# A hybrid S5, attention and expert layer: feature-major prologue, R on VectorE, x_mid stored and scaled by GpSimd

## The chip, the core and the metric

The kernel runs on one core of a Trainium2 chip. The metric is the device time of one execution in microseconds; less is better. TensorE (PE in the rows) does the matrix products, VectorE (DVE), ScalarE (ACT) and GpSimd (POOL) the element work, SyncE (SP) issues most transfers. An engine runs its instructions in the order in which they stand in its program; semaphores order the engines against each other.

## What is computed

```python
h  = modulate(rmsnorm(x), sh1, sc1)           # sh1, sc1, g1, sh2, sc2, g2 = silu(c) @ w_ada + b_ada
u, q_a, kv_a, k_r, gates = split(h @ w_in)    # for the 512 latent tokens x and the 256 context tokens ctx
# (a) two-way diagonal S5 scan over u (32 groups of 16 channels, 64 complex states each), then GLU
# (b) latent attention, 8 heads, over context and latent tokens
x_mid = x + g1 * (sigmoid(gates) * branches) @ w_out
h2  = modulate(rmsnorm(x_mid), sh2, sc2)
aff = softmax(h2 @ w_router)                  # 16 experts; each takes its 64 best tokens
out = x_mid + g2 * expert_choice_ffn(h2)      # SwiGLU with FF = 2816, scattered back by token
```

All in float32, D_MODEL = 1024, one sample. The experts' weights are about 554 MB of the 643 MB that the kernel moves.

## The kernel before

**Prologue.** Tokens lie as 8 slots `l` by 96 chunks (32 of ctx, 64 of x). SP loads `pk` (small constants), `X` (four tiles of 96 partitions, token-major), `craw` and `braw`, then the 16 pieces of `w_ada` for the first third (`wada`), then the first blocks of `w_in` (`win_u`, 128 columns each). ACT sums the squares of each row, DVE scales `X` by the norm, PE transposes it (L354, `xT`) into `xTa`, `xTb` (x, feature-major) and `hc` (ctx). PE forms the modulation `ada` (L191), `ada_end` moves it to columns (`adar`, `adac`, `acol`, `ab1`), and L632 to L643 make `h = x*a + b` per 128 features `k`, split as `hx` = (hi, lo) for products of three matmuls (`mm3`, L122 to L124). A weight block is split likewise into `ws` by `win_prep` (ACT, then one DVE subtraction).

**In-projection and S5.** Four `u` blocks (24 matmuls of 512 columns, and 16 of ctx, `pc`, L662) feed the S5 part; the other 21 blocks are "fills", put between the S5 steps to keep PE busy. The S5 loop runs over four group blocks `gb`. Per block: `s5_P` (tables `PT`, ten instructions, GpSimd), `s5_R` (powers `R`, about 20 instructions, GpSimd), `s5_Q` (tables `Q`, ten instructions, DVE), `s5_K` (matmuls `pkc` on `PT`, a round trip through `kd` in HBM, tile `M`), `s5_B` (transposes `pbt` of `Q`), `s5_V` (matmuls `pv`, DVE products with `R`, a scan, `Xc`), `s5_Y` (matmuls `py` on `M`, `PT`, `Xc`) and `s5_T`. `PT` and `R` have two buffers each, and P and R of block gb+2 follow Y of block gb on GpSimd. The stretch is under `manual_schedule`: written order is engine order. The in-projection ends at 307 us.

**Attention and router.** After MLA and attention, `pxm` gives `x_mid` in four token tiles `xm` and two column halves `n`. Each half is transposed (`pxt`, `xmT`) and multiplied with the router weights (`prt`: 4 products with a 128x128 stationary `xmT` and 16 columns). Tile by tile ACT stores `x_mid` to `out` (L1402, two DMAs a tile on ACT's queue) and then scales `xm` in place by the norm (L1405), for which it waits until the stores have landed. Then comes the top-k (8 rounds on DVE), and `pxg` gathers the rows of each expert from the scaled `xm`.

**Experts.** SP issues the weights of the 16 experts (L1450) into a ring of ten 2 MB slots, from 534 us on; each slot waits until PE has read its old content. The first expert's `pgu` starts at 625.73 us.

Of the kernel before, what the change touches and what calls it, by code (L numbers as in the profile page):

```python
# [18 lines left out]
D = 1024  # L19
SEQ = 512  # L20
# [36 lines left out]
def hybrid_block(ctx: ExitStack, tc: tile.TileContext, A, out, dbg=None, stop=99):  # L57
# [118 lines left out]
    win = A["w_in"].rearrange("(k p) n -> p k n", p=128)  # L176
    wada = A["w_ada"].rearrange("(k p) n -> p k n", p=128)
# [26 lines left out]
    def wada_src(t, kn, kh, q):  # L204
        return wada[:, kn * kh:kn * kh + kn, (4 * t + q) * 512:(4 * t + q + 1) * 512]


    pha = ph1.enter_context(ExitStack())
    for n, k in (("xx", 4), ("jk", 1)):
        cur[n] = pool(n, pha, bufs=k)  # L210
    man = ph1.enter_context(ExitStack())
    man.enter_context(tc.manual_schedule())
    xv = A["x"].rearrange("(c l) d -> c l d", l=L)
    cv = A["ctx"].rearrange("(c l) d -> c l d", l=L)
    X = []
    for j in range(4):
        t = tl("xx", f"X{j}", [NCH, 2, D])
        dma(t[0:NCX], cv[:, 2 * j:2 * j + 2, :])
        dma(t[NCX:NCH], xv[:, 2 * j:2 * j + 2, :])
        X.append(t)  # L220
    craw = cst("craw", [128, 2, 32, 16], p="early")
    dma(craw, A["ssm_c"])
    braw = tl("qq", "braw", [128, 2, 32, 16])
    dma(braw, A["ssm_b"])
    hc = tl("hxp", "hc", [128, 8, 256])
    wt = {}

# [12 lines left out]
    wada_load(2, [("m4", 0), ("m4", 0), ("rr", 0), ("rr", 0)])  # L240

# [55 lines left out]
    ssx = cst("ssx", [NCH, L])  # L297
    rstd = cst("rstd1", [NCH, L])
    for l in range(L):
        jk = tl("jk", "sqj", [NCH, D])  # L300
        S.activation(jk, X[l // 2][:, l % 2, :], AF.Square, accum_out=ssx[:, l:l + 1])
# [30 lines left out]
    def xnorm(hf):  # L332
        l0 = 4 * hf
        vx = sm("vx", [NCH, 4])
        ts(vx, ssx[:, l0:l0 + 4], 1.0 / D, EPS)
        yield
        yield from rsqrt_g(rstd[:, l0:l0 + 4], vx, [NCH, 4])
        for l in range(l0, l0 + 4):
            ts(X[l // 2][:, l % 2, :], X[l // 2][:, l % 2, :], rstd[:, l:l + 1])
            yield  # L340

    xt = []

    def xt_half(hf):
        if not hf:
            xt.extend([tl("pt", "xTa", [128, 4, 512]), tl("bt", "xTb", [128, 4, 512])])
        for kp in range(4):
            p = pw("xT")
            pv = p[:, :, 0:4 * NCH].rearrange("p k (l c) -> p k l c", l=4)
            k = 2 * kp  # L350
            for kk in range(2):
                for l in range(4):
                    lx = 4 * hf + l
                    T.transpose(pv[:, kk, l, :], X[lx // 2][:, lx % 2, 128 * (k + kk):128 * (k + kk) + 128],  # L354
                                ident[0:NCH, 0:NCH])
            S.copy(xt[k // 4][:, k % 4:k % 4 + 2, 256 * hf:256 * hf + 256].rearrange("p k (l c) -> p k l c", l=4),
                   pv[:, :, :, NCX:])
            V.tensor_copy(hc[:, k:k + 2, 128 * hf:128 * hf + 128].rearrange("p k (l c) -> p k l c", l=4),
                          pv[:, :, :, :NCX])
            for _ in range(4):  # L360
                yield
# [17 lines left out]
    lp = tl("uu", "lp", [128, 2, 9, 32])  # L379
# [7 lines left out]
    def powers():  # L387
        cm1 = sm("cm1", W32)
        stt(cm1, sh, -2.0, sh, ALU.mult, ALU.mult)
        yield  # L390
        ts(cb, cm1, 1.0, None, ALU.add)
        yield
        mul(nre, em1, cb)
        yield
        add(nre, nre, cm1)
        mul(lp[:, 0, 1], ex, cb)
        yield
        cmul(lp[:, :, 2:3], lp[:, :, 1:2], lp[:, :, 1:2], [128, 2, 1, 32], dtl)
# [5 lines left out]
        for o, m0, rev in ((lt_, 0, 1), (lq, 1, 0)):  # L404
            for dr in range(2):
                src = lp[:, :, m0:m0 + 8].rearrange("p r m (g d q) -> p g d r q m", d=2, q=4)[:, :, dr]
                dst = o.rearrange("p r (g d q) m -> p g d r q m", d=2, q=4)[:, :, dr]
                for g in range(4):
                    V.tensor_copy(dst[:, g], src[:, g, :, :, ::-1] if dr == rev else src[:, g])
                    yield  # L410
            if o is lt_:
                ts(lt_[:, 1], lt_[:, 1], -1.0)
# [71 lines left out]
    rr(expm1_parts(za, ex, em1), trig(), late_by(5, xnorm(0)))  # L484
    S.activation(sh, br, AF.Sin)
    S.activation(ch, ab, AF.Sin)
    rr(xnorm(1), late_by(2, powers2()), late_by(2, powers()), late_by(8, xt_half(0)))
    wada_load(3, [("zz", 0), ("xc", 0), ("xx", 1)])
    pada = pg("ada0")
    for k in range(2):  # L490
        ada_part(pada, k, [wt[0, q][:, k] for q in range(4)])
    rr(xt_half(1), rot(), late_by(8, bbar_g()))
    for k in range(2, 8):
        ada_part(pada, k, [wt[k // 2, q][:, k % 2] for q in range(4)])

# [104 lines left out]
    def win_load():  # L600
        if nxt["load"] < len(order):
            f, b = order[nxt["load"]]
            nxt["load"] += 1
            w = tl("raw", f"win_{f}{b}", [128, 8, 128])
            c = base[f] + 128 * b
            dma(w, win[:, :, c:c + 128])
            wins.append(w)

    def win_prep():

        if nxt["prep"] < len(order):
# [6 lines left out]
            if fb == ("u", 0):  # L618
                return
# [4 lines left out]
    for _ in range(4):  # L624
        win_load()
    wkr = tl("kr", "wkr", [128, 8, 32])
    dma(wkr, win[:, :, 1152:1184])
    ada_end(0, pada, tl("dt", "adar0", [128, 512]), win_prep)
# [88 lines left out]
    def f_kr():  # L719
# [12 lines left out]
        V.tensor_copy(kr4[:, 0:512], px)  # L732
        V.tensor_copy(kr4[:, 512:768], pc)
# [3 lines left out]
        V.tensor_copy(krt, pk_)  # L737
# [104 lines left out]
    win_prep()  # L842
    s5_Q(0)
    o = f_u(0)
    win_prep()
    u_out(0, *o)
# [792 lines left out]
```

## Time and profile before

| | us |
|---|---|
| median of 3 runs (range) | 1921.36 (1916.97 to 1926.43) |
| the profiled execution: its own time | 1919.85 |
| its span | 1918.1 |
| PE busy / DVE / ACT / POOL | 1633.8 / 531.5 / 320.7 / 209.9 |
| in-projection ends | 307 |
| top-k starts | 601.7 |
| first expert matmul | 625.73 |

The span is cut into stretches by what runs: 0 to 59 us prologue, 59 to 108 us the `u` blocks, to 307 us the S5 loop with fills, to 495 us MLA and attention, to 601 us `pmo`, `pxm` and router, to 626 us top-k and first gather, then the experts. The share of the longest chain is 43% PE, 36% DMA, 8% DVE. In a row of a timeline the brackets at the end tell how long the engine stood idle before it and what ended that.

### The profile page before, as it was taken

Reading aid. Unit: us, or ns where it says so; the run is one execution under the profiler, and the core shown is the slowest. Engines: PE = TensorE matmul, PEld = TensorE weight load, DVE = VectorE, ACT = ScalarE, POOL = GpSimd, SP = SyncE. Lnnn points to the kernel's source line nnn. Section 1 sums busy time; section 2 is a strip of 40 time slices with the busy share of each in tenths; the row PEclk is TensorE's granted clock in tenths of the full one; section 3 lists DMA queues with packets and bytes.
Section 4 is the critical chain, followed back from the end, with each engine's and each line's share of the span. In section 5 each row is a group of like instructions: output and inputs, shape, how many; then the busy total and the mean of one; then the engine's idle time right before and its main releaser. Section 6 shows DMA issues by size and latency. Waiting matters only on the chain.

```text
span 1918.1 us, 20921 instructions
## 1 busy us (share of the span) xinstructions
PE 1633.8 (85%) x8660; PEld 791.5 (41%) x8660; DVE 531.5 (28%) x1180; ACT 320.7 (17%) x593; POOL 209.9 (11%) x218
## 2 busy tenths in 40 slices
PE   3798999999995988888888888888888788888886
PEld 2586778755573333333333333323223232332322
DVE  7877665675745101011000100001000010100000
ACT  3422225364421000000000000000000000000000
POOL 3667200231110000000000000000000000000000
PEclk8899999999997999999999999999999999999999
DMA  9243353525539899999999999999999999999996
GB/s 316 57 141 111 105 189 133 170 97 201 157 90 401 363 422 426 422 427 420 422 427 422 421 426 422 426 423 423 425 421 427 421 427 421 420 428 421 427 422 281
DMA packets 108654, 642.56 MB, mean 335 GB/s; under 512 B 10256, under 2 KB 45072, under 8 KB 73232
## 3 DMA queue, kind: packets, MB, share of 16 engines
q1 hardware_dynamic: 105040, 631.79, 81.2%
q0 software_dynamic: 2880, 7.34, 1.7%
q10 hardware_dynamic: 640, 2.10, 0.3%
q8 instruction: 68, 1.11, 0.2%
q14 instruction: 26, 0.21, 0.0%
HBM read 623.93 MB, written 17.27 MB: 334 GB/s over the span
## 4 chain that ended last, share of the span: by engine, by line
PE 43%; DMA 36%; DVE 8%; issue 5%; ACT 3%; POOL 2%; POOLq 0%; ACTq 0%; SPq 0%; DVEq 0%
DMA wgu<-in_w_e_gu 18%; PE pgu L1505 14%; DMA wd<-in_w_e_down 10%; PE pdn L1520 8%; DMA wd<-in_w_e_down_end 6%; PE pxg L1462 2%; PE po L1263 1%; DVE hd L94 1%; PE px L122 1%; PE px L124 1%; PE px L123 1%; ACT hd L1507 1%; PE ada L191 1%; PE phT L1512 1%; PE py L801 1%
## 5 line engine op out<-in xcount | busy, mean ns | idle before, releaser
L1505 PE MATMUL pgu<-wgu,xe 128*64 128x512 f32 (+1 forms) x3072 | 644.9, 559 | 27.5 <-DMA wgu<-in_w_e_gu 26.0
L1505 PEld LDWEIGHTS pgu<-wgu,xe 128*64 128x64 f32 x3072 | 219.9, 137 | 426.5 <-issue 351.1
L1520 PE MATMUL pdn<-wd,hT 128*64 128x512 f32 x1408 | 357.5, 645 | 34.5 <-ACT hT L1514 34.5
L94 DVE TENSOR_TENSOR hd<-hd,pgu 64x512 f32<-64x512 f32 x96 | 61.9, 645 | 994.3 <-ACT hd L1507 994.3
L1507 ACT ACTIVATE hd<-pgu 64x512 f32<-64x512 f32 x96 | 53.3, 556 | 951.5 <-PE pgu L1505 951.5
L1520 PEld LDWEIGHTS pdn<-wd,hT 128*64 128x64 f32 x1408 | 110.9, 146 | 214.2 <-issue 163.6
L1539 POOL DMA_INDIRECT out<-ye,sidx x16 | 24.9, 1556 | 1340.7 <-DVE ye L112 1340.7
L1512 PE MATMUL phT<-pk,hd 64*128 64x64 f32 x352 | 42.1, 236 | 126.7 <-DVE hd L94 126.7
L1512 PEld LDWEIGHTS phT<-pk,hd 64*128 64x128 f32 x352 | 29.0, 138 | 204.3 <-DVE hd L94 204.3
L122 PE MATMUL px<-hx,ws 128*128 128x512 f32 x200 | 81.1, 406 | 6.3 <-ACT hx L637 6.3
L123 PE MATMUL px<-hx,ws 128*128 128x512 f32 x200 | 80.1, 400 | 3.5 <-DVE hx L94 3.4
L124 PE MATMUL px<-hx,ws 128*128 128x512 f32 x200 | 79.5, 398 | 1.4 <-DVE ws L94 1.4
L1462 PE MATMUL pxg<-xm,oh 128*64 128x512 f32 x256 | 75.3, 609 | 0.6 <-DVE oh L94 0.6
L1514 ACT COPY hT<-phT 128x256 f32<-128x256 f32 x96 | 34.1, 355 | 119.2 <-PE phT L1512 119.2
L122 PEld LDWEIGHTS px<-hx,ws 128*128 128x128 f32 x200 | 38.4, 192 | 15.3 <-ACT hx L637 6.4
L123 PEld LDWEIGHTS px<-hx,ws 128*128 128x128 f32 x200 | 38.1, 190 | 14.7 <-DVE hx L94 7.6
L124 PEld LDWEIGHTS px<-hx,ws 128*128 128x128 f32 x200 | 38.2, 191 | 10.2 <-DVE ws L94 2.5
L1466 DVE COPY xg<-pxg 128x256 f32<-128x256 f32 x16 | 6.8, 424 | 127.1 <-ACT xg L1465 127.1
L1462 PEld LDWEIGHTS pxg<-xm,oh 128*64 128x64 f32 x256 | 30.6, 140 | 21.1 <-issue 19.4
L1233 DVE TENSOR_REDUCE mx<-ps 128x1 f32<-128x768 f32 x32 | 30.5, 954 | 27.7 <-PE ps L124 25.0
L354 PE MATMUL xT<-pk,X 96*128 96x96 f32 x64 | 11.5, 348 | 29.1 <-DMA craw<-in_ssm_c 18.7
L191 PE MATMUL ada<-wada,scv 128*32 128x512 f32 x192 | 34.1, 675 | 0.0
(471 smaller groups left out, 1724.5 us busy)
## 6 DMA issues: line engine op xcount, KB each, us to landing
wgu<-in_w_e_gu SPq DMA_DIRECT2D x176, 2048.0 KB, 37.9
wd<-in_w_e_down SPq DMA_DIRECT2D x80, 2048.0 KB, 37.9
wada<-in_w_ada SPq DMA_DIRECT2D x16, 1024.0 KB, 7.7
wd<-in_w_e_down_end SPq DMA_DIRECT2D x16, 1024.0 KB, 36.8
wada<-in_w_ada SPq DMA_DIRECT2D x16, 512.0 KB, 10.6
win_g<-in_w_in SPq DMA_DIRECT2D x16, 512.0 KB, 4.3
gs<-gt SPq DMA_DIRECT2D x16, 256.0 KB, 2.0
g<-gs SPq DMA_DIRECT2D x16, 256.0 KB, 3.2
```

Of the source, the lines that this page charges most:

```text
L94: (e or V).tensor_tensor(o, a, b, op=op)
L122: T.matmul(o, a[0], b[0], start=first, stop=False)
L123: T.matmul(o, a[0], b[1], start=False, stop=False)
L124: T.matmul(o, a[1], b[0], start=False, stop=last)
L191: T.matmul(p[32 * q:32 * q + 32, :], scv[:, k].rearrange("p s n -> p (s n)"), w[q], start=(k == 0), stop=(k == 7))
L1233: V.tensor_reduce(mx, p[:, 0:768], AX.X, ALU.max, negate=True)
L1462: T.matmul(px[64 * h:64 * h + 64, :], oh[:, t], xms[t][:, 512 * h:512 * h + 512], start=(t == 0), stop=(t == 3))
L1505: T.matmul(p[64 * j:64 * j + 64, :fn], xe[:, k, :], wt_[8 * j + k], start=(k == 0), stop=(k == 7))
L1507: S.activation(hd[:, :fn], p[0:64, :fn], AF.Silu)
L1512: T.transpose(ph[:, b, :], hd[:, 128 * b:128 * b + 128], ident[0:64, 0:64])
L1514: S.copy(hT[:, :n], ph[:, :n])
L1520: T.matmul(po[64 * h:64 * h + 64, :], hT[:, b, :], w[:, 512 * h:512 * h + 512], start=(f0 == 0 and b == 0), stop=(f0 + 128 * b == FF - 128))
```

## The change

The host lays out x and ctx feature-major (`xt`, `ct`) and `w_ada`, `w_in` in blocks that are contiguous per partition. The transposes go; the norm comes from ACT squares, DVE sums, six matmuls `pssx` with a column of ones, and six matmuls `rb` that spread 1/rms over the partitions. `h` is then made per `k` from `xt`, `ab1` and `rb`, and the blocks u0 and u1 run together, `k` by `k`. R goes from GpSimd to DVE, behind Q; `PT` and `R` have one buffer, so P(gb+1) follows Y(gb). One fill stands ahead of the loop. In the router the weights are the stationary operand, in four column groups. `x_mid` is stored and scaled by GpSimd.

```diff
-    X = []
-    for j in range(4):
-        t = tl("xx", f"X{j}", [NCH, 2, D])
-        dma(t[0:NCX], cv[:, 2 * j:2 * j + 2, :])
-        dma(t[NCX:NCH], xv[:, 2 * j:2 * j + 2, :])
+    xt = [tl("pt", "xTa", [128, 4, 512]), tl("bt", "xTb", [128, 4, 512])]
+    for i in range(2):
+        for j in range(2):
+            k = 2 * j
+            dma(xt[i][:, k:k + 2, :], A["xt"][i, :, k:k + 2, :])
+        dma(hc[:, 4 * i:4 * i + 4, :], A["ct"][:, 4 * i:4 * i + 4, :])
...
+    win_load()
+    wada_load(3, ["m4", "m4", "zz", "xc"])
+    win_load()
+    win_load()
+    win_load()
+    braw = tl("qq", "braw", [128, 2, 32, 16])
+    dma(braw, A["ssm_b"])
...
+    for t in range(6):
+        T.matmul(rb[:, t // 4, 128 * (t % 4):128 * (t % 4) + 128], rstd[:, t:t + 1].to_broadcast([128, 128]), ident,
+                 start=True, stop=True)
...
+    h = modulated(0)
+    for k in range(8):
+        hi, lo = hxs(k)
+        S.activation(hi, h, AF.Identity, bias=ab1[:, 1, k, 0:1])
+        hn = modulated(k + 1) if k < 7 else None
+        if k:
+            hc_mod(k - 1)
+        stt(lo, h, ab1[:, 1, k, 0:1], hi.bitcast(F32), ALU.add, ALU.subtract)
+        h = hn
+        for j in range(2):
+            mm3(pf[:, j, :], [first[j][0][:, i, k, :] for i in range(2)], hxs(k), k == 0, k == 7)
...
     for gb in range(4):
         U, rt = us_.pop(gb)
+        s5_K(gb)
+        if gb < 3:
+            s5_bd(gb + 1)
         Xc = s5_V(gb, U, rt)
...
         if gb < 3:
             s5_Q(gb + 1)
+            s5_R(gb + 1)
         yb = s5_Y(gb, U, Xc)
         if gb < 3:
             us_[gb + 1] = s5_U(gb + 1)
-            s5_bd(gb + 1)
-        if gb < 2:
-            s5_P(gb + 2)
-            s5_R(gb + 2)
+            s5_P(gb + 1)
...
-            prt = pa("prt", (128, 16))
-            if n:
-                T.matmul(prt, ident, lg[:, t, :], start=True, stop=False)
+            prl = pa("prl", (128, 128))
             for k in range(4):
-                T.matmul(prt, xt_[:, k, :], wr[:, 4 * n + k, :], start=(n == 0 and k == 0), stop=(k == 3))
+                T.matmul(prl[32 * k:32 * k + 32, :], wr[:, 4 * n + k, :], xt_[:, k, :], start=True, stop=True)
...
+            prt = pa("prt", (128, 32))
+            T.matmul(prt, lgp[:, t], P("stack"), start=True, stop=True)
...
-                S.dma_start(ov[2 * t + i], xm[64 * i:64 * i + 64])
+                dmr(ov[2 * t + i], xm[64 * i:64 * i + 64])
 
     for t in range(4):
-        S.activation(xms[t], xms[t], AF.Copy, scale=inf[:, t, 1:2])
+        ts(xms[t], xms[t], inf[:, t, 1:2], e=G)
```

On PE the program began with the transposes between the modulation's products; these are its rows from the last transposes to the first block (`ada` the modulation, `adac` its columns, `px` a block).

```order
L354 MATMUL xT<-pk,X_152 128x96 x2
L191 MATMUL ada_427<-wada_166,scv 32x512 x2
L191 MATMUL ada_427<-wada_169,scv 32x512 x2
...
L191 MATMUL ada_427<-wada_424,scv 32x512 x2
L199 MATMUL adac_693<-pk,adar_689 128x8 x4
L122 MATMUL px<-hx_702,ws 128x512
```

The same place now: the sums `pssx` stand first, `rb` in the middle of the modulation.

```order
L370 MATMUL pssx<-ones,acc 128x1 x6
L190 MATMUL ada_432<-wada_164,scv 32x512 x2
L190 MATMUL ada_432<-wada_166,scv 32x512 x2
...
L513 MATMUL rb<-pk,rstd 128x128 x6
L190 MATMUL ada_432<-wada_172,scv 32x512 x2
...
L198 MATMUL adac_507<-pk,adar_505 128x8 x4
L123 MATMUL px_523<-hx_521,ws 128x512
```

The 64 transposes are gone, and the first block waits on `hx` after the same two steps of the modulation.

On DVE, in the first turn of the S5 loop, Q of block 1 stood ahead of the evictions of a fill (`kvo`) and of the gelu (`gl`).

```order
L94 TENSOR_TENSOR Q<-bbar,lq 128x1024
L94 TENSOR_TENSOR qu<-bbar,lq 128x512
L94 TENSOR_TENSOR Q<-Q,qu 128x512
L112 SCALAR_TENSOR_TENSOR kvo<-px,pk,kvo 128x512
L112 SCALAR_TENSOR_TENSOR kvo<-pc,pk,kvo 128x256
```

Now R of block 1 stands between them (`e` holds the powers that it multiplies with); 21 rows, of which these are the last.

```order
L604 COPY R<-e_221 128x16
...
L94 TENSOR_TENSOR cm_u<-R,e_221 128x256
L94 TENSOR_TENSOR cm_w<-R,e_221 128x256
L94 TENSOR_TENSOR R<-cm_u,cm_w 128x8x16 x2
L94 TENSOR_TENSOR cm_u<-R,e_221 128x512
L94 TENSOR_TENSOR cm_w<-R,e_221 128x512
L94 TENSOR_TENSOR R<-cm_u,cm_w 128x8x32 x2
```

What follows on DVE in that turn (`kvo`, the gelu, the next `ws`) moved behind R.

On ACT, in the router, the stores and the scaling stood between the steps that the next tile needs (`xg` squares of a half, `xmT` its transposes, `inf` the softmax).

```order
L1402 DMA out<-xm_4864 64x1024
L1393 ACTIVATE inf,res<-rlt,rmx 128x16
L1405 ACTIVATE xm_4863<-xm_4863,inf 128x1024
L1405 ACTIVATE xm_4864<-xm_4864,inf 128x1024
L1368 ACTIVATE xg_5290,ss_4874<-xm_4865 128x512
L1402 DMA out<-xm_4865 64x1024 x2
L1405 ACTIVATE xm_4865<-xm_4865,inf 128x1024
```

Now they are the last rows of GpSimd ahead of the scatter.

```order
L94 TENSOR_TENSOR wos<-w_out,wos 128x2048 x4
L1431 DMA out<-xm_4782 64x1024 x2
L107 TENSOR_SCALAR xm_4782<-xm_4782,inf 128x1024
L1431 DMA out<-xm_4783 64x1024 x2
L107 TENSOR_SCALAR xm_4783<-xm_4783,inf 128x1024
...
L107 TENSOR_SCALAR xm_4785<-xm_4785,inf 128x1024
L1568 DMA out<-ye,sidx 1024x512 x16
```

On ACT the squares of tile 3 (`xg` on the last `xm`) no longer stand behind the scaling of tiles 1 and 2; on GpSimd the stores of tile t+1 stand behind the scaling of tile t.

## Rows read from the trace of the kernel before

**Rows 1.** The chain that ended last: start us, us, what (router to first expert).
```profile
584.65 10.44 DMA out<-xm
...
617.38 5.34 PE pxg L1462 x16
...
625.73 10.51 PE pgu L1505 x46
```

**Rows 2.** Busy time by stretch; columns in the first line, clock granted to TensorE.
```profile
core 0: us, PE busy (x) PEld busy (x) DVE busy (x) ACT busy (x) POOL busy (x), PEclk, DMA share, GB/s
0.00:16.00 16.00, 0.00 (x0) 0.00 (x0) 6.33 (x48) 6.19 (x11) 0.73 (x5) 1.00 0.89 231
16.00:36.00 20.00, 12.10 (x64) 7.41 (x64) 19.44 (x84) 8.35 (x16) 6.60 (x4) 1.00 1.04 400
36.00:60.00 24.00, 11.65 (x73) 5.19 (x73) 23.32 (x81) 4.49 (x7) 18.11 (x28) 0.66 0.49 147
...
200.00:260.00 60.00, 56.06 (x507) 44.61 (x505) 44.23 (x74) 18.04 (x29) 6.11 (x9) 1.00 0.41 115
...
620.00:630.00 10.00, 8.35 (x52) 3.10 (x50) 2.33 (x11) 0.37 (x1) 0.00 (x0) 0.96 0.57 242
680.00:740.00 60.00, 51.43 (x252) 18.76 (x250) 4.34 (x8) 4.50 (x10) 1.68 (x1) 0.97 1.01 423
```

**Rows 3.** Timeline of PE, prologue and u blocks: start us, us, instruction, idle before.
```profile
44.00 6.98 PE L191 MATMUL ada<-wada,scv 128*32 128x512 f32 x48
51.70 1.06 PE L199 MATMUL adac<-pk,adar 128*128 128x8 f32 x8 [0.71 <-ACT adar L194]
59.09 0.80 PE L122 MATMUL px<-hx,ws 128*128 128x512 f32 x1 [6.34 <-ACT hx L637]
...
77.80 0.58 PE L122 MATMUL px<-hx,ws 128*128 128x512 f32 x1
...
83.44 3.61 PE L662 MATMUL pc<-hc,win_u 128*128 128x256 f32 x16
```

**Rows 4.** Timeline of PE: Y(0), Y(1) and Y(3) of the S5 loop.
```profile
122.33 0.44 PE L795 MATMUL py<-M,U 128*64 128x128 f32 x4
...
163.55 0.44 PE L795 MATMUL py<-M,U 128*64 128x128 f32 x4
...
259.31 0.44 PE L795 MATMUL py<-M,U 128*64 128x128 f32 x4
```

**Rows 5.** Timeline of DVE: Q(1), its first half without and its second beside GpSimd.
```profile
126.29 1.22 DVE L94 TENSOR_TENSOR Q<-bbar,lq 128x1024 f32<-128x1024 f32 x1
127.42 0.68 DVE L94 TENSOR_TENSOR qu<-bbar,lq 128x512 f32<-128x512 f32 x1
...
130.08 2.96 DVE L94 TENSOR_TENSOR Q<-bbar,lq 128x1024 f32<-128x1024 f32 x1
...
139.23 0.74 DVE L112 SCALAR_TENSOR_TENSOR kvo<-px,pk,kvo 128x512 fp32r<-128x512 f32 x1
```

**Rows 6.** Timeline of POOL: the first of P(2), the first and last of R(2).
```profile
129.89 2.06 POOL L94 TENSOR_TENSOR PT<-craw,lt 128x1024 f32<-128x1024 f32 x1
...
146.86 0.11 POOL L575 MEMSET R<- 128x8 f32 x1
...
162.75 3.19 POOL L94 TENSOR_TENSOR R<-cm_u,cm_w 128x256 f32<-128x256 f32 x2
```

**Rows 7.** Timeline of PE: a router product between `pxm` matmuls.
```profile
578.86 0.96 PE L1378 MATMUL prt<-wr,xmT 128*128 128x16 f32 x8
```

**Rows 8.** Timeline of ACT and DVE: scaling and squares of the last tiles.
```profile
595.20 1.15 ACT L1405 ACTIVATE xm<-xm,inf 128x1024 f32<-128x1024 f32 x1 [5.35 <-DMA out<-xm]
...
596.25 0.61 ACT L1368 ACTIVATE xg<-xm 128x512 f32<-128x512 f32 x1
```

**Rows 9.** The tile `out` up to 620 us: its stores and their landing.
```profile
L1402 ACTq DMA_DIRECT2D out<-xm x8: 473/476/619, 569.3 to 595.8; - x8
...
DMA to landing us min/median/max: 3.4/6.1/11.8
```

More of the change, by code (lines that the diff above doesn't have):

```diff
@@ new lines, in hybrid_block, with wada_load @@
+    wt = {}
+    def wada_load(kh, tags):
+        n = len(tags)
+        for i, tag in enumerate(tags):
+            t = tl(tag, f"wada{kh}{i}", [128, 4 // n, 2, 512])
+            dma(t, wada_src(0, kh, 4 // n * i, 4 // n))
+            for j in range(4 // n):
+                wt[kh, 4 // n * i + j] = t[:, j]
+    wada_load(0, ["hxp", "hxp"])
+    wada_load(1, ["hxp", "hxp"])
+    wada_load(2, ["ws", "ws"])
+    order = [(f, b) for f, bs in (("u", range(4)), ("g", (0, 1, 2)), ("kv", (0,)), ("g", (3, 4, 5)), ("kv", (1,)),
+                                  ("g", (6, 7, 8)), ("q", (0, 1)), ("g", (9, 10)), ("q", (2,)), ("g", range(11, 16)))
+             for b in bs]
@@ L330, in trig, with xnorm @@
         yield
[L332 to L335, printed above, removed]
-        yield
[L337 to L361, printed above, removed]
+    rstd = cst("rstd", [128, 6])
+    def xnorm():
+        pss = pa("pssx", (128, 6))
+        for t in range(6):
+            T.matmul(pss[:, t:t + 1], acc[:, 128 * t:128 * t + 128], ones, start=True, stop=True)
+        for _ in range(9):
+            yield
+        ssx = sm("ssx", [128, 6])
+        ts(ssx, pss, 1.0 / D, EPS)
+        yield
+        yield from rsqrt_g(rstd, ssx, [128, 6])
     def cmul(o, a, b, shape, mk=None, e=None):
@@ L403, in powers, with spread @@
         yield
[L404 to L412, printed above, removed]
+    def spread(o, m0, rev):
+        for dr in range(2):
+            src = lp[:, :, m0:m0 + 8].rearrange("p r m (g d q) -> p g d r q m", d=2, q=4)[:, :, dr]
+            dst = o.rearrange("p r (g d q) m -> p g d r q m", d=2, q=4)[:, :, dr]
+            for g in range(4):
+                V.tensor_copy(dst[:, g], src[:, g, :, :, ::-1] if dr == rev else src[:, g])
+                yield
+        if o is lt_:
+            ts(lt_[:, 1], lt_[:, 1], -1.0)
     def powers2():
@@ L622, in win_prep @@
                 win_load()
[L624 to L628, printed above, removed]
+    win_prep()
+    ada_end(0, pada, tl("dt", "adar0", [128, 512]))
     ab1 = cst("ab1", [128, 2, 8, 2])
@@ L842, in hybrid_block @@
     win_prep()
-    s5_Q(0)
-    o = f_u(0)
-    win_prep()
-    u_out(0, *o)
-    us_ = {0: s5_U(0)}
-    o = f_u(1)
-    win_prep()
-    u_out(1, *o)
-    s5_B(0)
+    win_prep()
+    us_ = {}
+    for b in range(2):
+        pc = ctx_block(first[b][1])
+        win_load()
+        u_out(b, pf[:, b, :], pc)
+        if b == 0:
+            us_[0] = s5_U(0)
+    rr(bbar_g())
+    s5_Q(0)
+    rr(spread(lt_, 0, 1))
+    s5_P(0)
     o = f_u(2)
-    s5_bd(0)
     win_prep()
     u_out(2, *o)
-    s5_K(0)
-    s5_P(1)
-    s5_R(1)
+    s5_R(0)
     o = f_u(3)
@@ L935, in t_ysp, with t_ysps @@
             ysp.append([s[:, 0, i], s[:, 1, i]])
+    def t_ysps():
+        for j in range(2):
+            t_ysp(j)
     gr = P("grope").rearrange("p (a e) -> p a e", a=4)
@@ L1278, in a_ada @@
         for k in range(4):
[L1279 removed]
+            ada_part(ads["p"], 4 * (hp % 2) + k, [wt[hp][q][:, k // 2, k % 2] for q in range(4)])
             yield
```

194 lines of the change are left out of this document (98 added, 96 removed).

## The prediction

> **What bounds the kernel now.** I read the chain of waits first. From the first expert's `pgu` at 625.73 us to the end it alternates between PE and weight transfers. Is the weight stream late or early at that point? The stretch 620 to 630 us moves 242 GB/s at a DMA share of 0.57, the steady stretch behind it 423 GB/s at 1.01 [rows 1, 2]: the ring of weights is full when `pgu` starts and waits for PE. So the end of the kernel follows the start of `pgu` one for one, as long as the ring is still full there. The rest is about the 626 us ahead of it.
>
> Second, the prologue. PE does nothing in the first 16 us, then works in pieces; the modulation ends at 44.00 + 6.98 = 50.98 us, its columns at 52.8, and the first block starts at 59.09, behind ACT and a DVE that is busy 23.32 of 24 us [rows 2, 3]. The u blocks and their ctx parts u0 and u1 end at 83.44 + 3.5 = 87 us. DMA moves only 231 GB/s in the first 16 us and 400 in the next 20 [rows 2].
>
> Third, the S5 loop. Y(0) is at 122.33, Y(1) at 163.55 (41.2 us), Y(3) at 259.31: 137.0 us for three turns [rows 4]. PE is busy 56.06 of 60 us there and DVE 44.23 [rows 2]; both are near their limit, PE nearer.
>
> Fourth, the router. The chain passes through the landing of a store, 584.65 to 595.1, because ACT waits 5.35 us to scale a tile and only then squares the last one [rows 1, 8].
>
> **The prologue.** Ahead of the last piece of the modulation stand 3 MB of x and ctx, 8 MB of w_ada, a block of w_in and the constants, 12.1 MB. At 400 GB/s that is 30 us and some 3.5 us of start, 33.5 us; at the mean of the first 36 us, (16 x 231 + 20 x 400)/36 = 325 GB/s, 37 us; at 423 GB/s from time 1, 30 us. I take 33.5, nearer to the 400 row: the slow 16 us are those of 32- and 64-partition loads, which go. The last 16 products cost 6.98/48 x 16 = 2.3 us: the modulation ends at 35.8 us. Then the copy (0.7), `adac` (1.06), three small DVE operations, one subtraction of 128x1024 (1.22, [rows 5]), the first `h` (0.68, the form of `qu`) and ACT's hi (0.8, an estimate a little above the 0.61 of `xg`) give a first block at 41 us instead of 59.09: **18 us earlier**, 13 to 20 with the two ends. Where the old start waited for both ACT and DVE, what is late next is DVE: per `k` it makes h and lo, 2 x 0.68 = 1.4 us, against 6 matmuls at 5.64/24 = 0.235, 1.4 us too [rows 3]. At full clock u0 and u1 take 11.3 us, at half clock 22 (the clock was 0.66 here, [rows 2]); I take 13, so 54 us, and two ctx parts of 3.5 us end at 61, where 87 stood.
>
> From there the PE stays ahead but another engine becomes late. u2 and u3 (5.64 + 3.5 each) end at 79, B(0) at 82, one fill at 87. Meanwhile DVE, done with u0/u1 and their subtractions at 57.5, makes `bbar` (eight forms of 128x512 or half, and small ones: 6.4 us), Q(0) (2 x (1.22 + 4 x 0.68) = 7.9 us) and the spread of `lt` (1), to 73. Only then P(0) can start on GpSimd; P(2) took 146.86 - 129.89 = 17.0 us beside DVE [rows 6], so P(0) ends at 90, and PE waits about 3 us for it. With a round trip of `kd` beside `pv` and the scan (V) Y(0) comes at 106 (103 to 109) instead of 122.33: 16.4 us earlier, and with one fill of 5.64 us already done.
>
> **The loop.** R leaves GpSimd and costs DVE: eight instructions near the 0.68 form of `qu` and a dozen smaller ones that I put at 0.2, 8 us a turn. DVE's share of 44.23/60, in a stretch in which GpSimd is nearly still (6.11 us), is 33.7 us for a mean turn of 45.7 [rows 2, 4]; with R that is 41.7, less the `kr` copies that ACT takes over, 41 us. Collisions with GpSimd come on top. They are seen in Q(1): its second half took 139.23 - 130.08 = 9.15 us beside P(2) for 1.22 + 4 x 0.68 = 3.9 us of work, 2.3 times as long [rows 5, 6]. In the new order R and Q stand ahead of Y and P behind it, so P meets the gelu, the subtractions and the head of V: about half of its 17 us, some 7 us a turn: 48. PE's own work sets no less than the 45.7 that a turn has taken. Three turns of 48 make 144 against 137.0: **7 us lost**. Behind Y(3) one fill less remains: 5.6 us. The in-projection ends 16.4 + 5.6 - 7 = 15 us earlier; I take 13, since the lower clock of the prologue may come back in the 3 us gap. With no collisions it is 22, with all of them (below) about 0.
>
> The rule of the Trainium skill, SBUF — State Buffer, section Who interferes with whom, speaks here: a DVE instruction with two inputs in SBUF and a GpSimd instruction that reads SBUF exclude each other for the whole instruction, so they would run one after the other. The trace agrees: in the 9.15 us Q's 3.9 us and about 6 of P's went by. By it R on DVE is no bare cost either, as R on GpSimd (19 us beside DVE's V) took the same port.
>
> **The router.** Seven `prt` groups of 0.96 us stand on PE's path between `pxm` matmuls [rows 7]; with four column groups side by side a group should take 0.35 (the 16-column products go four at a time, as the modulation's 0.145 each did [rows 3]), with 0.2 for the added stack product on four tiles: 7 x 0.6 - 0.8 = **3 us gained** (0 to 4.4). ACT no longer waits: the squares of tile 3 could start at 591 instead of 596.25 [rows 8], 5.2 us. Against it, GpSimd stores and scales in a chain: two issues, landing, a scaling of about 2 us, four times; `pxg` needs the last. The old landings are 3.4 to 11.8, median 6.1 [rows 9]; at 11.8 a round is 1.2 + 11.8 + 2 = 15 us, four from 569 end at 629, while the gather, 5 us earlier, wants them from 612 on, tile by tile [rows 1]. At 6.1 the chain is hidden. I take **3 us gained** net (-6 to 5.2).
>
> Sum: 13 + 3 + 3 = 19 us from the profiled execution's 1919.85 gives **1901 us**. That execution lies 1.5 us under the median, within the spread of the three runs; I leave the 1901. The measurement can tell about 0.5%, 9.6 us, from no change, so faster means below 1911.75.
>
> **The rivals.**
>
> *DVE becomes the bound of the loop.* For it: DVE at 44.23 of 60 already, 8 us a turn added. If all of P (two instructions of 2.06 and eight of half that, 12.4 us [rows 6]) falls on DVE's path, a turn is 41 + 12.4 = 53.4, three turns 160, 16 us more than my 144: **1917 us**. Against it: V waits for `pv` part of the time, and P then runs free. The rule of the Trainium skill named above is this rival's mechanism if it holds for every pair that meets.
>
> *The stores and scalings on GpSimd are late: slower.* Place: `out` and `xm` between 569 and the gather. Price: each round over 15 us pushes the last scaling by four times the excess. In the times of the old trace the gather reaches tile 3 at three quarters of `pxg`, 617.38 + 4 = 621.4 [rows 1]. It eats the 16 us of prologue, loop and `prt` only if the last scaling ends 16 later, at 637.4: rounds of 17.1 us, that is pair landings of 13.9, above the largest seen, 11.8. At 20 us a round, 569 + 80 = 649: 27.6 us late, less 16 gained: **1931 us**. For it: weights now fill the queues at the same time; GpSimd issues the descriptors itself. Against it: the median of 6.1. The same section of the Trainium skill warns of transfers issued by GpSimd, whose descriptors starve while DVE holds the port; no row here shows it, and the sum goes without it.
>
> *The ring is not yet full.* If the weights do not come earlier with PE, the gain is capped where the old ring was full, shortly before 625.7: the 242 GB/s of 620 to 630 say that some 4 of 10 us were spare. Loads are issued when their slots and queues allow; the first tiles wait behind stores of `out` today, and would no longer. If only the router's part is capped, gain 15: **1905 us**.
>
> *Better.* No collisions in the loop and the loads at 423 GB/s: 19 + 7 + 4 = 30 us, **1889 us**.
>
> **How the numbers follow.** My case 0.62, DVE-bound 0.18, ring 0.08, better 0.07, late stores 0.05. The first, third and fourth are faster, 0.77; DVE-bound counts as same, 0.18; slower 0.05. My own case reaches from 1893 to 1909; the range to the better case and the DVE case, 1888 to 1915, leaves out the late stores and some of each tail.
>
> **What would show it.** First `px` at 41 us and Y(0) at 106: prologue right; at 50 and 116 it is wrong. Y(3) at 250: loop right; DVE busy over 90% between the Ys and PE waiting on `Xc` or `pkc`: the DVE rival. The end of the in-projection at 294. Squares of tile 3 within a microsecond of the last `xm` on DVE; `pxg` waiting on POOL `xm`: the store rival. A DMA share of 1 in the 10 us around the first `pgu`: the ring rival. I am wrong if the first block's earlier start is given back before 300 us.

## The result, and the profile after

The changed kernel takes 1937.24 us (median of four runs, 1935.95 to 1939.31) against 1920.62 for the kernel before (four runs): a ratio of 1.0087, interval 1.007 to 1.0104. It is 0.9% slower, where 1901 us was forecast. The profiled execution took 1935.95 us, with a span of 1934.2.

| us | before | after | forecast |
|---|---|---|---|
| first `px` | 59.09 | 41.81 | 41 |
| Y(0) | 122.33 | 109.82 | 106 |
| Y(1) | 163.55 | 164.66 | 154 |
| Y(3) | 259.31 | 281.58 | 250 |
| in-projection ends (first lo product of `pkv`) | 307.0 | 323.3 | 294 |
| top-k ends (`psel`) | 614.0 | 625.1 | - |
| first `pgu` | 625.73 | 645.81 | 607 |
| from there to the end of the span | 1292.4 | 1288.4 | as before |

The prologue, with all that stands ahead of the loop, gave its gain: at Y(0) the changed kernel is 12.5 us ahead. Three turns of the loop then take 171.8 us instead of 137.0 and lose 34.8; the tail gets back 6.0; attention and router get back 5.2; the gather loses 9.0; the experts get back 4.0. -12.5 + 34.8 - 6.0 - 5.2 + 9.0 - 4.0 = 16.1 us, the difference of the spans.

The timeline of PE in the changed kernel, start and length in us, shows Y(0), Y(1), Y(2) and Y(3), which answer to [rows 4]. The first bracket is a wait of 3.9 us that the forecast did not have. It is put down to the store of a gate block, but what `py` reads is `M` and `U`. `U` had been read by `pv` at 90.31 us already; the eight loads of `M` were issued from 103.4 to 107.0 us and took 2.2 to 2.9 us to land. So this is the round trip of `M` through HBM.

```profile
109.82 0.69 PE L811 MATMUL py<-M,U 128*64 128x128 f32 x4 [3.92 <-DMA gs<-gt]
...
164.66 0.44 PE L811 MATMUL py<-M,U 128*64 128x128 f32 x4
...
227.94 0.44 PE L811 MATMUL py<-M,U 128*64 128x128 f32 x4
...
281.58 0.44 PE L811 MATMUL py<-M,U 128*64 128x128 f32 x4
```

What PE waited for between 59 and 325 us, changed kernel (total us, times, longest):

```profile
PE pkr L742 <- DVE kvo L112: 12.7, 1, 12.7
PE pbt L566 <- DVE msum L703: 11.1, 1, 11.1
PE px L122 <- DVE kvo L112: 9.8, 1, 9.8
```

These are one wait in each turn, 33.6 us together. In all three PE stands still until VectorE has evicted a fill's block (`msum` in the second row stands behind such an eviction). The old turns had waits too, so the account goes by busy time. First the old loop, Y(0) to Y(1) and Y(1) to Y(3), then the three new turns and the 6.3 us behind the first of the waits (columns as in [rows 2]):

```profile
122.33:163.55 41.22, 40.40 (x350) 32.60 (x349) 34.94 (x42) 13.02 (x21) 32.47 (x37) 1.00 0.45 125
163.55:259.31 95.76, 86.10 (x746) 66.83 (x745) 68.01 (x104) 26.07 (x41) 29.95 (x41) 0.96 0.37 108
```

```profile
109.82:164.66 54.84, 44.45 (x349) 35.97 (x349) 46.01 (x73) 10.19 (x18) 13.72 (x11) 0.85 0.29 90
164.66:227.94 63.28, 48.74 (x410) 35.98 (x409) 47.23 (x75) 13.98 (x24) 15.39 (x11) 0.87 0.27 82
227.94:281.58 53.64, 39.63 (x338) 31.61 (x337) 48.69 (x76) 12.02 (x18) 15.45 (x11) 0.87 0.33 96
139.68:146.00 6.32, 6.32 (x20) 5.06 (x21) 3.34 (x6) 1.58 (x2) 0.00 (x0) 0.71 0.39 140
```

PE's idle time rose from 10.5 to 39.0 us: that is 28.5 of the 34.8 us. The other 6.3 us are matmuls that ran longer, 132.8 us busy instead of 126.5 for nearly the same count, at a granted clock of 0.85 to 0.87 where the old turns had 1.00 and 0.96. So a standstill costs more than its own length. Behind the first of the three the granted clock is 0.71, between its two levels of 1.2 and 2.4 GHz, and `px` starts again with matmuls of 0.63 us instead of 0.39. Behind the 3.9 us ahead of Y(0) it is 0.63 (109.82 to 118.20), and Y(0) takes 8.5 us up to the copy of its result instead of 6.1. So why was VectorE late? Its timeline in the first turn, from the end of Q(1) to that eviction, has the answer:

```profile
119.74 0.69 DVE L94 TENSOR_TENSOR Q<-Q,qu 128x512 f32<-128x512 f32 x1
120.38 1.88 DVE L604 COPY R<-e 128x16 f32<-128x16 f32 x1
...
122.30 0.99 DVE L94 TENSOR_TENSOR cm_u<-R,e 128x32 f32<-128x32 f32 x1
123.21 0.18 DVE L94 TENSOR_TENSOR cm_w<-R,e 128x32 f32<-128x32 f32 x1
...
125.88 3.03 DVE L94 TENSOR_TENSOR R<-cm_u,cm_w 128x32 f32<-128x32 f32 x2
...
134.87 0.69 DVE L94 TENSOR_TENSOR cm_u<-R,e 128x512 f32<-128x512 f32 x1
...
138.88 0.74 DVE L112 SCALAR_TENSOR_TENSOR kvo<-px,pk,kvo 128x512 fp32r<-128x512 f32 x1
```

R takes 138.88 - 120.38 = 18.5 us. Up to 134 us its smallest instructions are the dear ones: 1.88 us for 16 columns, 3.03 for two of 32. From 134.87 on, 512 columns cost 0.69, as in [rows 5]. GpSimd's timeline in the same time gives the first and the last instruction of P(1):

```profile
119.75 2.47 POOL L94 TENSOR_TENSOR PT<-craw,lt 128x1024 f32<-128x1024 f32 x1
122.19 1.05 POOL L94 TENSOR_TENSOR pu<-craw,lt 128x512 f32<-128x512 f32 x1
...
132.43 1.26 POOL L94 TENSOR_TENSOR PT<-PT,pu 128x512 f32<-128x512 f32 x1
```

P(1) runs from 119.75 to 133.7, the dear part of R. P itself is hardly slowed: its rows of 512 columns take 1.05 to 1.39 us, and the whole 14, where P(2) took 17 before [rows 6].

In the other two turns P comes earlier against VectorE, at 172.92 and 236.19 us, and meets the second half of Q as well. These are VectorE's rows in the second turn:

```profile
176.21 1.43 DVE L94 TENSOR_TENSOR Q<-Q,qu 128x512 f32<-128x512 f32 x1
...
180.73 1.21 DVE L604 COPY R<-e 128x16 f32<-128x16 f32 x1
...
194.97 0.74 DVE L112 SCALAR_TENSOR_TENSOR kvo<-px,pk,kvo 128x512 fp32r<-128x512 f32 x1
```

Q takes 11.9 us there instead of 7.6 in the first turn, and R 14.2 and 14.3.

In the router, GpSimd's timeline from the first store to the last scaling:

```profile
585.93 1.14 POOL L1431 DMA_DIRECT2D out<-xm  x2 [27.59 <-DVE xm L94]
597.68 2.85 POOL L107 TENSOR_SCALAR xm<-xm,inf 128x1024 f32<-128x1024 f32 x1 [10.60 <-PE prtT L1427]
600.49 1.15 POOL L1431 DMA_DIRECT2D out<-xm  x2
...
625.32 1.14 POOL L1431 DMA_DIRECT2D out<-xm  x2
636.97 2.83 POOL L107 TENSOR_SCALAR xm<-xm,inf 128x1024 f32<-128x1024 f32 x1 [10.52 <-DMA out<-xm]
```

Four rounds take 53.9 us, 13.5 in the mean; three of the four scalings waited 10.5 to 10.6 us, one 6.4. In the first row of a scaling the releaser is put down to PE, but `inf` of tile 0 had long been there; it was the landing, as the last row says. On PE the gather waits for it, and the last tile's products follow the scaling at once:

```profile
628.56 4.22 PE L1491 MATMUL pxg<-xm,oh 128*64 128x512 f32 x12 [0.66 <-DVE oh L94]
639.86 1.97 PE L1491 MATMUL pxg<-xm,oh 128*64 128x512 f32 x4 [7.08 <-POOL xm L107]
```

### The profile page after: what moved, and what is told of

It is laid out like the page before. It is cut to its first block, busy times and chain, and to the rows that moved or that the text cites. A ratio compares the mean times of both kernels' runs of the same rounds, so it can differ in the third digit from the quotient of the medians.

```text
span 1934.2 us, 20830 instructions
## 1 busy us (share of the span) xinstructions
PE 1634.0 (84%) x8620; PEld 786.9 (41%) x8620; DVE 570.5 (29%) x1278; ACT 310.8 (16%) x580; POOL 158.1 (8%) x122
## 4 chain that ended last, share of the span: by engine, by line
PE 42%; DMA 36%; DVE 12%; issue 5%; ACT 3%; POOL 1%; POOLq 0%; SPq 0%; ACTq 0%; DVEq 0%
DMA wgu<-in_w_e_gu 20%; PE pgu L1534 15%; PE pdn L1549 8%; DMA wd<-in_w_e_down 6%; DMA wd<-in_w_e_down_end 6%; PE pxg L1491 2%; PE po L1288 1%; DVE hd L94 1%; DMA wada<-in_w_ada 1%; DMA out<-xm 1%; ACT hd L1536 1%; DVE Q L94 1%; PE px L122 1%; DVE R L94 1%; PE px L123 1%
## 5 line engine op out<-in xcount | busy, mean ns | idle before, releaser
L1534 PE MATMUL pgu<-wgu,xe 128*64 128x512 f32 (+1 forms) x3072 | 645.7, 561 | 19.8 <-DMA wgu<-in_w_e_gu 18.5
L124 PEld LDWEIGHTS px<-hx,ws 128*128 128x128 f32 x200 | 38.5, 193 | 11.1 <-DVE ws L94 2.9
L1261 ACT ACTIVATE pr<-ps,mx 128x768 f32<-128x768 f32 x32 | 28.9, 903 | 10.8 <-DVE mx L1258 5.9
## 6 DMA issues: line engine op xcount, KB each, us to landing
wgu<-in_w_e_gu SPq DMA_DIRECT2D x176, 2048.0 KB, 36.6
wd<-in_w_e_down SPq DMA_DIRECT2D x80, 2048.0 KB, 36.6
wd<-in_w_e_down_end SPq DMA_DIRECT2D x16, 1024.0 KB, 36.6
```

What stands on the lines that cost most here:

```text
L124: T.matmul(o, a[1], b[0], start=False, stop=last)
L1534: T.matmul(p[64 * j:64 * j + 64, :fn], xe[:, k, :], wt_[8 * j + k], start=(k == 0), stop=(k == 7))
```

## The experiments

### The place of R on VectorE (e1_r_late)

```diff
             s5_Q(gb + 1)
-            s5_R(gb + 1)
...
         s5_out(gb, t, y)
+        if gb < 3:
+            s5_R(gb + 1)
```

> R(gb+1) stands behind the gelu of block gb on VectorE instead of ahead of the fill's eviction. Theory (R meets P on GpSimd, each of its small instructions waits for a whole one of P's, and the evictions kvo stand behind it, so PE waits 9.8, 12.7 and 11.1 us): kvo at about 125 instead of 138.9 us, the three waits below 2 us each, Y(0) to Y(3) 140 to 147 us instead of 171.8, first pgu near 618, time 1908 to 1916. Rival (what was moved besides, K at the head of the turn and one buffer of PT, makes the turns long): Y(0) to Y(3) stays above 165 us, time above 1930.

Measured: 1911.23 us (five runs), a ratio to before of 0.9953 (0.9921 to 0.9985). Y(0) to Y(3) is 109.61 to 252.05, 142.4 us; the first `pgu` comes at 620.5. The three waits for evictions are gone from the list of PE's waits; these lead it:

```profile
PE px L124 <- DVE ws L94: 6.1, 4, 4.1
PE py L811 <- DMA gs<-gt: 5.0, 2, 3.1
PE py L817 <- DVE Xc L94: 4.2, 4, 1.6
```

The eviction starts at 128.43 instead of 138.88 us (125 was expected), and R, at 132.57, meets only the last of P: it takes 9 us. K's new place, the single buffers and R on VectorE are all still there; together what they cost the loop is within the 5.4 us by which it is still longer than the old one (142.4 against 137.0), besides the 3 us for `M` ahead of Y(0), and the kernel is faster than before.

### Collision or queue? (e2_p_after_r)

```diff
             us_[gb + 1] = s5_U(gb + 1)
+            G.tensor_copy(tl("ptmp", "pd", [128, 2, 8, 1]), RTs[gb + 1][:, :, :, 95:96])
             s5_P(gb + 1)
```

> The order on VectorE stays; GpSimd reads one column of R(gb+1) before it starts P(gb+1), so that P can't run beside R. Theory (collision): R takes 8 us instead of 18, kvo comes at 129 instead of 138.9, PE's waits shrink by 8 to 10 us each, partly replaced by a wait for P, which ends near 143: Y(0) to Y(3) 145 to 152 us instead of 171.8, time 1914 to 1922. Rival (the place of R in VectorE's queue costs, collision or not): the waits shrink by 3 us at most, Y(0) to Y(3) above 162, time above 1929.

Measured: 1920.95 us (ten runs), ratio 1.0002 (0.9991 to 1.0013), so 16 us better than the changed kernel with VectorE's order untouched. On VectorE the first rows of R and the eviction behind it are now:

```profile
120.83 0.17 DVE L604 COPY R<-e 128x16 f32<-128x16 f32 x1
...
121.37 0.26 DVE L94 TENSOR_TENSOR R<-cm_u,cm_w 128x16 f32<-128x16 f32 x2
...
128.65 0.74 DVE L112 SCALAR_TENSOR_TENSOR kvo<-px,pk,kvo 128x512 fp32r<-128x512 f32 x1
```

The copy that took 1.88 us beside P takes 0.17, and R 7.8 us instead of 18.5. PE's wait for `kvo` shrinks to 3.0 us in all. So nearly all of the cost is the collision, not the place in the queue. The three turns take 155.3 us, 3 more than the upper end of what was expected, because the delayed P is itself waited for:

```profile
PE pkc L581 <- POOL PT L94: 10.0, 4, 4.2
```

### R back on GpSimd (e3_r_gpsimd)

```diff
-        V.memset(R[:, 0, :, 0:1], 1.0)
+        G.memset(R[:, 0, :, 0:1], 1.0)
...
-            cmul(R[:, :, :, n:n + e], ..., [128, 2, 8, e], dtl)
+            cmul(R[:, :, :, n:n + e], ..., [128, 2, 8, e], lambda nm, s: tl("ptmp", nm, s), G)
```

> R back on GpSimd, in the new place (ahead of P(gb+1)), one buffer each. Theory (R on VectorE is the loss): R starts when V has read the old one, takes 16 to 19 us beside Q, P ends near 143; PE's waits for kvo go, Y(0) to Y(3) 140 to 150 us, time 1910 to 1918. Rival (K's place and the single buffers): Y(0) to Y(3) above 165, time above 1930. A third: GpSimd in a row (R 19 and P 14 to 17 us) makes PE wait for PT at pkc, 5 us a turn, Y(0) to Y(3) 155 to 160.

Measured: 1938.77 us (four runs), ratio 1.0093 (1.0062 to 1.0123). From the first `py` of Y(0) to that of Y(3) it takes 168.9 us. Time and length are the rival's, above 1930 and 165, but the waits are those of the third outcome: R and P in a row on GpSimd run from 116.8 to 152.6 us in the first turn, and PE waits for `PT`:

```profile
PE pkc L581 <- POOL PT L94: 21.6, 7, 5.9
PE py L818 <- DVE Xc L94: 11.2, 2, 9.9
```

The 9.9 us stand inside Y(0), between its first two steps: there R(0) comes behind P(0) on GpSimd, and V waits for it. What speaks against the rival is e1, which has K's place and the single buffers too and runs in 142.4 us. So with one buffer each, R on GpSimd costs as much as the collision did (1938.77 against 1937.24); before, P(gb+2) and R(gb+2) had a whole turn more.

### The store queue (e5_act_store, e4_act_store_scale)

```diff
-                dmr(ov[2 * t + i], xm[64 * i:64 * i + 64])
+                S.dma_start(ov[2 * t + i], xm[64 * i:64 * i + 64])
```

> The stores of x_mid go back to ScalarE's queue, the scaling stays on GpSimd. Theory (on GpSimd each pair of stores is issued only after the tile before has landed and been scaled, landings of 10.5 to 10.9 us in a row up to 636.97): all stores out by about 611, last scaling ends near 627 instead of 639.8, the gather no longer waits for xm (7.1 us), first pgu near 638 instead of 645.8, time 1929 to 1931. Rival (a store lands late wherever it is issued, because the weights fill the queues): last scaling after 634, gain under 3 us, time 1933 to 1936.

Measured: 1930.91 us (seven runs), ratio 1.0052 (1.0031 to 1.0074). The last scaling ends at 621.56 + 2.85 = 624.4 instead of 639.8 us, and the gather does not wait. But the top-k ends 2.2 us later (627.3; why, no run shows), so that the first `pgu` comes at 640.4: 5.4 us gained of the 8 expected.

The second kernel gives the scaling back to ScalarE too.

```diff
-        ts(xms[t], xms[t], inf[:, t, 1:2], e=G)
+        S.activation(xms[t], xms[t], AF.Copy, scale=inf[:, t, 1:2])
```

> Stores and scaling of x_mid both go back to ScalarE; all else as changed. Theory (the chain of pair landings on GpSimd costs 8 us ahead of the first expert): the top-k starts some 5 us later than in the changed kernel, as ScalarE waits for a landing ahead of the last tile's squares, the gather then waits for nothing, first pgu near 642 instead of 645.8, time 1932 to 1935. Rival (stores land late on any queue and the scaling waits as long): first pgu at 645 to 650, time 1936 to 1941.

Measured: 1932.89 us (four runs), ratio 1.006 (1.004 to 1.008); the top-k ends at 631.6, 6.5 us later than in the changed kernel, and the first `pgu` is at 644.6. This is the old trade: ScalarE waits for a landing ahead of the last tile, and the gather then waits for nothing. The whole GpSimd part of the change is worth 4 us of loss in this kernel.

### One part alone in the kernel before (e9_before_pool_store)

> The kernel before with one part of the change alone: x_mid stored and scaled by GpSimd. Theory: the top-k starts 5 us earlier (596.5 instead of 601.7), but the chain on GpSimd, 54 us from the first store to the last scaling in the changed kernel, ends at about 623 to 628; the gather waits for it, first pgu at 628 to 632 instead of 625.7, time 1922 to 1927. Rival (the chain is hidden here): first pgu at 620.5, time 1915 to 1917.

The edits are those two, the other way round, in the kernel before. Measured: 1923.52 us (ten runs), ratio 1.0014 (0.9998 to 1.003). The top-k ends at 606.1 us, 7.9 earlier than before (2.1 of it came ahead of the router), the last scaling ends at 617.5, and the gather waits only 2.8 us for it. First `pgu` at 623.3: between the two expectations. Alone, this part changes nothing that can be told. The profiled execution has a granted clock of 0.944, and from the first `pgu` to the end it takes 1298.0 us instead of 1292.4. Three of its four rounds took 14 to 15 us, one 7; why, no run shows.

### The scaled one-hot (e8_scaled_onehot, e7_late_onehot, e10_first_onehot)

The gather needs xm divided by its rms. Instead of scaling xm one can scale the one-hot matrix:

```diff
-    for t in range(4):
-        ts(xms[t], xms[t], inf[:, t, 1:2], e=G)
...
+        ohs = l2("ohs", [128, 4, 64])
+        mul(ohs, oh, inf[:, :, 1:2].to_broadcast([128, 4, 64]))
```

> xm isn't scaled in place; the one-hot matrix that gathers the rows is multiplied by 1/rms instead (one VectorE product of 128x256 for each expert), so nothing waits for the stores to land. They stay on GpSimd, one behind the other without a scaling between. Theory: the gather follows the top-k at once, from the end of the top-k to the first pgu 12.5 us instead of 20.7, first pgu near 637.5, time 1927 to 1930. Rival (the gather is late for another reason, the lower clock or the weights): first pgu above 643, time above 1933.

Measured: 1941.68 us (four runs), ratio 1.0114 (1.0093 to 1.0135): slower, though the first `pgu` comes at 640.2, 5.6 us earlier. From there to the end it takes 1298.5 us instead of 1288.4. With R's repair on top:

> R(gb+1) behind the gelu, and the scaled one-hot: both repairs. Theory (the two losses add, and the end follows the first pgu one for one): first pgu at 620.5 - 8 = 612.5, time 1901 to 1905. Rival (the ring of weights is no longer full when pgu starts that early): first pgu at 612 but time 1905 to 1911.

Measured: 1913.5 us (nine runs), ratio 0.9962 (0.9949 to 0.9976); first `pgu` at 610.3, then 1298.3 us. The rival named a ring that is too empty, but PE no longer waits for `wgu`, weights of the experts, at all, where it waited 22.4 us in e1. Its waits from 600 us on have one new entry:

```profile
PE pxg L1491 <- DVE ohs L94: 8.5, 15, 1.3
```

In sum PE waits less than in e1 and still takes 9.2 us longer from the first `pgu`: it is busy for 1120.6 us there instead of 1093.4. All nine runs have a mean granted clock of 0.945 to 0.948, four of e1's five 0.960 to 0.964. So the gain was given back to the lower clock. The profiled execution of e9, without any such product, shows the same at 0.944: 1298.0 us, and no wait for `wgu`. Whether the product ahead of every gather brings that clock is asked in e11. To avoid it, only the first gather should use the scaled one-hot:

```diff
+        ohs = oh
+        if e == 0:
+            ohs = l2("ohs", [128, 4, 64])
+            mul(ohs, oh, inf[:, :, 1:2].to_broadcast([128, 4, 64]))
...
     nxt_ = gather(0)
+    for t in range(4):
+        ts(xms[t], xms[t], inf[:, t, 1:2], e=G)
```

> R(gb+1) behind the gelu; only the first expert's gather uses the scaled one-hot, then GpSimd scales xm in place for the other 15. Theory (the scaled one-hot of every expert made PE wait 8.5 us in 15 pieces and left the experts at the lower clock; the first gather alone brings the gain): first pgu at 610 us, 1289 to 1292 us from there to the end, time 1900 to 1904. Rival (a first pgu this early finds the ring of weights too empty, whatever the gathers do): first pgu at 610, but 1296 to 1299 us from there, time 1908 to 1912.

Measured: 1901.7 us (four runs), ratio 0.9892 (0.9856 to 0.9929). This is the best kernel of the study, 1.1% faster than before; its granted clock is 0.954 to 0.966. The first `pgu` comes at 614.4 (four us later than expected, the top-k ends at 600.8 instead of 597.2 in the kernel ahead of it), and from there it takes 1286.7 us. The four scalings now lie in one row behind the first gather, with no store between them:

```profile
583.30 1.09 POOL L1432 DMA_DIRECT2D out<-xm  x2 [5.93 <-DVE xm L94]
607.05 11.33 POOL L107 TENSOR_SCALAR xm<-xm,inf 128x1024 f32<-128x1024 f32 x4 [22.66 <-issue]
```

### Do the two repairs add? (e6_late_act_store)

The edits of e1 and e5 together.

> R(gb+1) behind the gelu, stores on ScalarE's queue, scaling on GpSimd. Theory (the two gains add: 25.3 us of R's place and 5.4 us of the store queue): first pgu at 614 to 616 us, time 1904 to 1907. Rival (they don't add, since the stores then meet the weight stream at another moment): first pgu at 618 to 621, time 1908 to 1912.

Measured: 1904.11 us (four runs), ratio 0.9908 (0.9872 to 0.9943), first `pgu` at 611.7. They add: 33.1 us under the changed kernel, where e1 has 26.0 and e5 6.3.

### The pause ahead of the gathers (e11_before_pause)

```diff
+        ohs = l2("ohs", [128, 4, 64])
+        mul(ohs, oh, ones[:, None, :].to_broadcast([128, 4, 64]))
```

> The kernel before, with one extra VectorE product of 128x256 ahead of each gather (the one-hot times one; the result is the same). Theory (a pause of 0.57 us for PE ahead of each gather makes PE the bound of the experts and its clock lower): PE waits 8.5 us for ohs and hardly for wgu, granted clock 0.94 to 0.95 in all runs, time 1924 to 1930. Rival (the level of the clock comes and goes by itself; the pauses are taken from PE's 26 us of waits for weights): clocks as in the kernel before, 0.963 in most runs, time 1919 to 1923.

Measured, in the kernel before: 1927.79 us (ten runs), ratio 1.0027 (1.0008 to 1.0045). All ten runs have a mean granted clock of 0.941 to 0.947; of the 13 runs of the kernel before beside them nine are at 0.956 to 0.965 and four at 0.944 to 0.947. The stretches of this kernel (columns as in [rows 2]) show the same engine at 0.98 early and 0.93 later:

```profile
640.00:720.00 80.00, 70.46 (x352) 24.84 (x350) 7.70 (x21) 5.84 (x13) 1.68 (x1) 0.98 1.00 414
1200.00:1400.00 200.00, 172.31 (x808) 61.06 (x808) 18.29 (x48) 14.56 (x32) 3.09 (x2) 0.93 1.01 423
```

The second of these stretches in the kernel before, and in e9, which has no pause either:

```profile
1200.00:1400.00 200.00, 170.00 (x826) 62.44 (x824) 18.56 (x55) 13.97 (x31) 3.09 (x2) 0.97 1.01 424
1200.00:1400.00 200.00, 175.29 (x836) 64.86 (x834) 17.92 (x51) 13.97 (x31) 3.10 (x2) 0.94 1.01 424
```

PE's 26 us of waits for `wgu` are gone, as in e7 and e8, and as in e9. So a pause of 0.57 us ahead of each gather goes with the lower clock, in ten runs of ten against four of 13. How it does so is open, and a pause is not the only way there: without one, four of the ten runs of e9 have 0.940 to 0.948 and all four of e3 0.939 to 0.946. Most of the 7 us go with the clock: the four runs of the kernel before at 0.944 to 0.947 have a median of 1925.2 us, the nine others 1920.3.

## Why the prediction was wrong

**What bounds the kernel: right, but for 4 us.** The end followed the first `pgu`: in the profiled executions with a granted clock of 0.95 or more (the changed kernel, e1, e2, e4, e5, e6, e10) it takes 1286.7 to 1291.3 us from there, over 34 us of shift. In those under 0.95 (e3, e7, e8, e9, e11) it takes 1294.8 to 1298.5. Before it was 1292.4 at 0.965. Why the changed kernel got 4 us back is open: e1 and e10 got them too, with a first `pgu` earlier than the old one, so a ring that had more time to fill is not the reason. The ring rival's sign did not show: from 639.86 to 645.80 us the DMA share is 0.01.

**The prologue: right in mechanism and size.** The modulation ended at 36.95 against 35.8, the first block came at 41.81 against 41. Y(0) came 3.8 us later than forecast. The 3 us that PE was to wait for P(0) did not come (P(0) ended at 88.3, and `pkc` followed the fill at 89.30); the 3.9 us of that first bracket did, since I had put the round trip of `M` beside V, at no cost. No run changes the prologue alone: its gain is read from the profiles.

**The loop: the step that failed.** It reads: "In the new order R and Q stand ahead of Y and P behind it, so P meets the gelu, the subtractions and the head of V: about half of its 17 us, some 7 us a turn: 48." I took an order between two engines for an order in time. Y runs on PE, and all it needs from VectorE is `Xc`, which is done at 110.5; while PE ran Y(0), from 109.8 to 118, VectorE was at Q(1) until 120.4. P(1), which follows Y(0), started at 119.75, and R(1) at 120.38. They met head on, and in the next two turns P met the second half of Q too. The size failed with it: R has 17 small instructions, the copy and 16 products; I had put a dozen at 0.2 us, and many of them waited for about one whole instruction of P's, 1.05 to 2.5 us. The term "R 8 us" was right without the collision (7.8 in e2) and 18.5 with it; Q and R together lost 10.7 us in the first and second turn and 10.8 in the third, where 7 stood.

The second half of the failed step is what the 48 stood for. VectorE's busy time came out near it, 47.3 us a turn, but with a larger collision and a smaller rest (36.6 where 41 stood), which is luck. But I took the longer of two busy times for the length of a turn. PE was busy for 44.3 us of a turn and VectorE for 47.3, and the turn took 57.3: behind R stand the evictions, for which PE waited 33.6 us in three turns, and those waits were put at nothing. My own sign, an earlier start given back before 300 us, showed: Y(3) came 22.3 us later than in the kernel before.

The trace agrees with the rule of the Trainium skill, SBUF — State Buffer, section Who interferes with whom: the two-input products of 32 columns took 3.03 us for a pair beside P and 0.30 in e2 without it. I had cited it and then priced it only for the pairs that I thought would meet. The copy at the head of R, which has one input, waited as well, 1.88 us against 0.17.

The rival "DVE becomes the bound of the loop", at 1917, came nearer: it let all of P fall on VectorE's path, 12.4 us a turn, for turns of 53.4 us. But its signs showed only in part. VectorE was busy for 84, 75 and 91% of the three turns and not over 90% throughout, and PE waited for evictions and not for `Xc` or `pkc`. The turns came to 57.3 us because the two engines waited for each other.

**The router: half right.** A `prt` group fell from 0.96 to 0.43 us, and the squares of the last tile started at 606.81, right behind `xm` on VectorE (606.71). The top-k came 5.2 us earlier relative to the in-projection, of the 8.2 at most that the two terms gave. The step "At 6.1 the chain is hidden" failed in its 6.1: three of four pairs landed about 10.5 us after their issue, near the 11.8 of [rows 9], a scaling took 2.84 us instead of 2, and rounds of 13.5 us ended at 639.8, 14.7 us after the top-k: 7.1 us of wait in the gather. Of the 9.0 us that the gather lost the rest went by behind this wait, where the granted clock is 0.50, the lower of its two levels (639.86 to 645.80 us). The net is a loss of 3.8, where 3 gained stood. The rival of the late stores needed rounds of 17 us to make the kernel slower by itself; rounds of 13.5 took 3.8, and e9 shows no loss that can be told from this part alone.

Keeping P and R apart is not enough for the forecast: e2 does only that and measures 1920.95 us, above the range of 1888 to 1915. e1, which also takes R out of the way of the evictions, measures 1911.23, within it. That e10 comes to 1901.7, beside the forecast of 1901, is chance: its repair of the gather was no part of the change that was forecast.

## What to carry to other kernels

When work moves to another engine, lay both engines' timelines against each other by release times, not by program order: what frees the buffer, when, and what is the other engine doing then? Price a collision by the number of instructions that can wait, not by the work they do; small ones lose most. Put work that nobody waits for behind the evictions that the bound engine waits for, and don't let a store's landing stand between two steps of a queue when the first user can scale the data on its way instead. Only the first: the same product ahead of every gather gave the gain back (e7, e8).

## What the runs showed of the hardware

- Beside a GpSimd product with operands in SBUF, a VectorE copy of 16 columns took 1.88 us instead of 0.17 and a pair of products of 32 columns 3.03 instead of 0.30, while GpSimd's products of 512 columns kept 1.05 to 1.39 in that turn.
- GpSimd scales 128x1024 in 2.84 us, ScalarE in 1.15 [rows 8].
- Behind PE's standstills of 9.8, 12.7 and 11.1 us the granted clock was 0.71, 0.55 and 0.50 in the next stretch (139.68 to 146.00, 195.77 to 202.00, 259.17 to 266.00 us); behind the first, `px` matmuls of 512 columns took 0.63 us instead of 0.39.
- Executions of one and the same kernel have different mean granted clocks: 0.944 to 0.947 in four of 13 runs of the kernel before, 0.956 to 0.965 in the others, with medians of 1925.2 and 1920.3 us.
- With a pause of 0.57 us ahead of each of 15 gathers, 8.5 us, all ten runs had 0.941 to 0.947 and the median was 7 us longer, although PE had waited 26 us for weights in the same stretch. How the pause and the clock hang together is open.
